# Newton steps of the first norm in runs of late priority, more buffers and one table load less, in a four-layer decoder trunk

## Chip, cores and metric

The kernel runs on one NeuronCore of one Trainium2 chip, as one program for the whole network. The metric is the device time of one execution in microseconds. Engines are named as the profile names them: PE (TensorE, with PEld for its weight loads), DVE (VectorE), ACT (ScalarE), POOL (GpSimd) and SP (SyncE, which issues the DMAs).

## What is computed

Four decoder layers of width 1024 on a sequence of 256 tokens, batch 1, all in float32. Every layer has two SwiGLU feed-forwards of half weight (hidden width 2816) around one mixer; the mixers are stick-breaking attention, MoBA, MLA and stick-breaking attention again. Cut to what matters here:

```python
def rms_norm(x, g):
    y = x * lax.rsqrt(jnp.mean(x * x, axis=-1, keepdims=True) + EPS)
    return y * g

def swiglu(x, w_gate_up, w_down):
    g, u = jnp.split(x @ w_gate_up, 2, axis=-1)
    return (jax.nn.silu(g) * u) @ w_down

h = x
for i in range(DEPTH):
    h = h + 0.5 * swiglu(rms_norm(h, norm_ffn1[i]), ffn1_w_gate_up[i], ffn1_w_down[i])
    h = h + mixer[i % 3](rms_norm(h, norm_mix[i]))
    h = h + 0.5 * swiglu(rms_norm(h, norm_ffn2[i]), ffn2_w_gate_up[i], ffn2_w_down[i])
return rms_norm(h, final_norm)
```

## The kernel before

Activations lie transposed in SBUF, features on the 128 partitions and the 256 tokens along the free axis; `h` has eight such tiles. To keep float32 accuracy at the fast matmul rate, every operand is split in two: a high part (rounded to fp32r) and a low part (what is left over). For activations they are the two halves of `x2`. For weights, `Chunk` loads up to 2048 columns into one of four `raw` buffers (SP, L315), ACT writes the high part `whi` (L320) and DVE the low part `wlo` (L327), 1024 columns at a time, into one of six pairs of part buffers (`parts`). One step of a product, here called a wide pair, is two matmuls: high weight by both halves of the activation (L478, 512 columns) and low weight by the high half (L479, 256 columns). One pair of part buffers of the gate-and-up projection feeds eight wide pairs: four contraction tiles into two PSUM banks.

A feed-forward walks over 22 groups of 128 hidden units, each with two part pairs of gate and up weights, and then over eight output tiles of the down projection. The evacuation of a group (`evac`) adds the two halves of each bank (ACT L486, DVE L487), multiplies by the row scale (L554), takes SiLU (ACT L555), multiplies (L559) and splits the result (ACT L560, DVE L561). It holds one of three intermediate buffers (`mids`) all that time.

The row scale `rb` is made by `norm_rows`: a matmul sums the squares (`sums`, L444 and L445, one wide pair), and DVE finds the reciprocal root with a first guess (L450, L451) and three Newton steps of three instructions each (L454 to L456). These eleven are one operation, `newton`. The norm gains are applied to the activations beforehand, so the matmuls don't wait for `rb`; the evacuation does.

What sets the order: every piece of work is registered as an operation with a cost, its dependencies and a priority, which is the PE time planned so far (`g.t`) minus a `lead`. `Program.emit` then plays the program through with these costs, and on each engine takes the ready operation with the lowest priority number for which buffers are free. The instructions are emitted in that order, one in-order row per engine. A higher lead means earlier. `norm_rows` has lead 10.

At the start, ACT runs a SiLU on one element (L266), which brings its function table in; the planned work then begins with a table load of its own (`table`, L467). The first three groups of weights come in small cuts.

Of the kernel before, what the change touches and what calls it, by code (L numbers as in the profile page):

```python
# [11 lines left out]
F32R = mybir.dt.float32r  # L12
BF16 = mybir.dt.bfloat16
I32 = mybir.dt.int32
AF = mybir.ActivationFunctionType
ALU = mybir.AluOpType
AX = mybir.AxisListType

P = 128
D = 1024  # L20
SEQ = 256
# [7 lines left out]
ZC = SEQ + P  # L29
EPS = 1e-6  # L30
# [9 lines left out]
HALF = MAXC // 2  # L40
# [155 lines left out]
def trunk_kernel(ctx: ExitStack, tc: tile.TileContext, a: dict, out: bass.AP, nsub: int = 3 * DEPTH):  # L196
    nc = tc.nc
# [23 lines left out]
    def room(n, shape, name, dt=F32):  # L221
        return Slots([cp.tile([P] + shape, dt, name=f"{name}{i}") for i in range(n)])
# [2 lines left out]
    raws = room(4, [MAXC], "raw")  # L225


    whi = [cp.tile([P, HALF], F32R, name=f"whi{i}") for i in range(6)]
    full = cp.tile([P, P], F32R, name="full")
    cp.tile([P, 16], F32, name="shift")  # L230

    x2 = cp.tile([P, NT, 2, SEQ], F32R, name="x2")
    a2 = cp.tile([P, NF, 2, SEQ], F32R, name="a2")
    lows = cp.tile([P, 4 + P + 6 * HALF], F32R, name="wlo")
    full_lo = lows[:, 4:4 + P]
    parts = Slots([(whi[i], lows[:, 4 + P + i * HALF:4 + P + (i + 1) * HALF]) for i in range(6)])
    mids = room(3, [2 * ZC], "mid")
    probs = room(2, [2, ZC], "prob")
    nats = room(5, [512], "nat")
    turned = room(4, [4, SEQ], "turned")  # L240
# [22 lines left out]

    zeros = nats.aps[0].bitcast(BF16)
    nc.vector.memset(nats.aps[0], 0.0)
    nc.scalar.activation(nats.aps[1][:, 0:1], nats.aps[0][:, 0:1], AF.Silu)  # L266
    for _ in range(WARM):
        nc.tensor.matmul(psum.aps[-1], zeros[:, :P], zeros[:, :512], start=True, stop=True)

# [154 lines left out]
        p = g.op("PE", 0.22, spread, [n], take=[c], lead=lead)  # L424
        return r, n, [g.act(SEQ, copy(i, s), [p], free=[c], lead=lead) for i, s in enumerate(scales)]

    def norm_rows():

        t, z = Buf(mids), bank()
        lead = 10.0

        parted = a2[:, NF - 1].rearrange("p a b -> p (a b)")
        th, tl, tx = (slice(i * SEQ, (i + 1) * SEQ) for i in range(3))

        def high():
            nc.scalar.activation(parted[:, th], acc, AF.Copy)

        def low():  # L440
            nc.vector.tensor_sub(parted[:, tl], acc, parted[:, th].bitcast(F32))

        def sums():
            nc.tensor.matmul(z.ap, full, parted, start=True, stop=False, skip_group_check=True)  # L444
            nc.tensor.matmul(z.ap[:, :SEQ], full_lo, parted[:, tl], start=False, stop=True, skip_group_check=True)  # L445

        def newton():
            x, y, u = t.ap[:, tx], t.ap[:, th], t.ap[:, tl]

            nc.vector.tensor_scalar(x, z.ap[:, :SEQ], 0.5 / D, -0.5 * EPS, op0=ALU.mult, op1=ALU.add)  # L450
            nc.vector.tensor_scalar(y.bitcast(I32), x.bitcast(I32), -0.5, float(0x1EF759DF), op0=ALU.mult,  # L451
                                    op1=ALU.add)
            for i in range(3):
                nc.vector.tensor_mul(u, y, y)  # L454
                nc.vector.tensor_mul(u, u, x)
                nc.vector.scalar_tensor_tensor(rb[:, 0, :] if i == 2 else y, u, 1.5, y, op0=ALU.add, op1=ALU.mult)  # L456

        o = g.act(SEQ, high, [state["acc"]], lead=lead)
        o = g.dve(SEQ, low, [o], lead=lead)
        o = g.op("PE", wide_cost(1), sums, [o], take=[z, t], lead=lead)  # L460
        n = g.op("DVE", 11 * 0.4, newton, [o], free=[z, t], lead=lead)
        g.act(SEQ, lambda: nc.scalar.activation(rb[:, 1, :], rb[:, 0, :], AF.Copy, scale=0.5), [n], lead=lead)
        return n

# [61 lines left out]

    def ffn(l, which, g_next):
        gu, dn = a[f"ffn{which + 1}_gu"], a[f"ffn{which + 1}_dn"]
        rms = norm_rows()
        act = [None] * NF  # L530
        xdeps = list(state["x"])

# [38 lines left out]
        for m in range(NT):  # L571
            b = bank()
            last = None
            for half in range(2):
                c = Chunk(dn[l, m, half], FH, P, 6)
                for fs in runs(FH, 3):
                    def f(fs=fs, half=half, c=c, b=b):
                        for f in fs:
                            j = half * FH + f
                            wide(b.ap, *c.get(f), a2[:, j], j == 0, j == NF - 1)  # L580
# [504 lines left out]
```

## Time and profile before

| | us |
|---|---|
| median of 3 runs | 1920.49 |
| the runs | 1920.95, 1915.59, 1920.49 |
| profiled execution | 1913.88 |
| its span in the profile | 1911.8 |
| PE busy | 1893.1 (99%) |
| DVE busy | 1467.3 (77%) |
| ACT busy | 1150.4 (60%) |

The span runs from the first to the last instruction; the 2.1 us by which the execution is longer lie around it. Matmuls overlap in the array, so the busy time of PE has no gap as long as one follows the other, and its rate is better read from the number of matmuls in a stretch. In a waits row, the engine named first sat idle until the second had delivered.

### The profile page before, as it was taken

Reading aid. Unit: us, or ns where it says so; the run is one execution under the profiler, and the core shown is the slowest. Engines: PE = TensorE matmul, PEld = TensorE weight load, DVE = VectorE, ACT = ScalarE, POOL = GpSimd, SP = SyncE. Lnnn points to the kernel's source line nnn. Section 1 sums busy time; section 2 is a strip of 40 time slices with the busy share of each in tenths; the row PEclk is TensorE's granted clock in tenths of the full one; section 3 lists DMA queues with packets and bytes.
Section 4 is the critical chain, followed back from the end, with each engine's and each line's share of the span. In section 5 each row is a group of like instructions: output and inputs, shape, how many; then the busy total and the mean of one; then the engine's idle time right before and its main releaser. Section 6 shows DMA issues by size and latency. Waiting matters only on the chain.

```text
span 1911.8 us, 30484 instructions
## 1 busy us (share of the span) xinstructions
PE 1893.1 (99%) x11649; PEld 1674.1 (88%) x11649; DVE 1467.3 (77%) x2670; ACT 1150.4 (60%) x2119; POOL 0.4 (0%) x5
## 2 busy tenths in 40 slices
PE   8999999999999999999999999999999999999997
PEld 6888989888888887988888888988888888898886
DVE  8777767876887777887787768887778777669874
ACT  6655556655656555755665657765656655666653
POOL 0000000000000000000000000000000000000000
PEclk9999999999999999999999999999999999999999
DMA  7546434545654653364655454255465456335542
GB/s 270 197 152 223 176 132 155 206 171 190 227 188 153 219 190 132 135 219 158 207 213 194 157 188 159 104 208 190 166 222 197 175 180 225 145 113 212 181 164 83
DMA packets 55873, 342.77 MB, mean 179 GB/s; under 512 B 6192, under 2 KB 7088, under 8 KB 26928
## 3 DMA queue, kind: packets, MB, share of 16 engines
q1 hardware_dynamic: 55728, 340.84, 51.3%
q8 instruction: 91, 1.49, 0.3%
q14 instruction: 54, 0.44, 0.1%
HBM read 339.76 MB, written 1.05 MB: 178 GB/s over the span
## 4 chain that ended last, share of the span: by engine, by line
PE 98%; DVE 1%; ACT 1%; DMA 0%; SPq 0%; issue 0%; DVEq 0%; ACTq 0%
PE ps L478 50%; PE ps L479 25%; PE ps L472 3%; PE ps L473 3%; PE ps L474 3%; PE ps L519 3%; PE ps L521 2%; PE ps L520 2%; PE ps L618 1%; PE ps L668 1%; PE ps L777 1%; PE ps L742 1%; PE ps L815 1%; PE ps L640 1%; PE ps L606 0%; PE ps L620 0%
## 5 line engine op out<-in xcount | busy, mean ns | idle before, releaser
L320 ACT ACTIVATE whi<-raw 128x1024 fp32r<-128x1024 f32 (+2 forms) x738 | 703.0, 954 | 659.6 <-PE ps L478 461.0
L327 DVE TENSOR_TENSOR wlo<-raw,whi 128x1024 fp32r<-128x1024 f32 (+2 forms) x738 | 803.0, 1090 | 334.8 <-ACT whi L320 315.8
L478 PE MATMUL ps<-x,whi 128*128 128x512 f32 x2816 | 962.3, 390 | 1.4 <-ACT whi L320 1.4
L479 PE MATMUL ps<-x,wlo 128*128 128x256 f32 x2816 | 779.3, 277 | 4.4 <-DVE wlo L327 4.4
L478 PEld LDWEIGHTS ps<-x,whi 128*128 128x128 f32 x2816 | 530.1, 188 | 113.2 <-ACT whi L320 2.7
L479 PEld LDWEIGHTS ps<-x,wlo 128*128 128x128 f32 x2816 | 530.0, 188 | 5.6 <-DVE wlo L327 5.5
L478 PE MATMUL ps<-a,whi 128*128 128x512 f32 x1408 | 480.1, 389 | 0.0
L479 PE MATMUL ps<-a,wlo 128*128 128x256 f32 x1408 | 388.6, 276 | 0.0
L478 PEld LDWEIGHTS ps<-a,whi 128*128 128x128 f32 x1408 | 264.3, 188 | 54.7
L479 PEld LDWEIGHTS ps<-a,wlo 128*128 128x128 f32 x1408 | 264.3, 188 | 0.0
L487 DVE TENSOR_TENSOR mid<-ps,mid 128x256 f32<-128x256 f32 x416 | 172.9, 417 | 10.0 <-ACT mid L486 9.9
L486 ACT ACTIVATE mid<-ps 128x256 f32<-128x256 f32 x416 | 151.0, 368 | 12.9 <-PE ps L479 9.9
L559 DVE TENSOR_TENSOR mid<-mid 128x256 f32<-128x256 f32 x176 | 73.9, 422 | 11.7
L554 DVE TENSOR_TENSOR mid<-mid,rb 128x256 f32<-128x256 f32 x176 | 74.1, 423 | 4.8
L555 ACT ACTIVATE mid<-mid 128x256 f32<-128x256 f32 x176 | 72.0, 410 | 7.2 <-DVE mid L554 7.2
L561 DVE TENSOR_TENSOR a<-mid,a 128x256 fp32r<-128x256 f32 x176 | 73.2, 418 | 1.1 <-ACT a L560 0.8
L519 PE MATMUL ps<-whi,x 128*128 128x512 f32 (+2 forms) x192 | 74.0, 385 | 0.0
L472 PE MATMUL ps<-a,whi 128*128 128x256 f32 x256 | 73.8, 288 | 0.0
L472 PE MATMUL ps<-x,whi 128*128 128x256 f32 x256 | 73.1, 285 | 0.0
L521 PE MATMUL ps<-whi,x 128*128 128x512 f32 (+2 forms) x192 | 72.8, 379 | 0.0
L520 PE MATMUL ps<-wlo,x 128*128 128x512 f32 (+2 forms) x192 | 72.3, 377 | 0.0
L560 ACT ACTIVATE a<-mid 128x256 fp32r<-128x256 f32 x176 | 70.6, 404 | 2.4 <-DVE mid L559 1.9
(142 smaller groups left out, 1660.2 us busy)
## 6 DMA issues: line engine op xcount, KB each, us to landing
raw<-in_ffn_gu SPq DMA_DIRECT2D x173, 1024.0 KB, 4.8
raw<-in_ffn_dn SPq DMA_DIRECT2D x128, 704.0 KB, 4.0
raw<-in_sb_qk SPq DMA_DIRECT2D x16, 1024.0 KB, 4.8
raw<-in_moba_qkv SPq DMA_DIRECT2D x12, 1024.0 KB, 4.7
raw<-in_sb_v SPq DMA_DIRECT2D x8, 1024.0 KB, 4.8
raw<-in_sb_o SPq DMA_DIRECT2D x8, 1024.0 KB, 4.8
raw<-in_moba_o SPq DMA_DIRECT2D x4, 1024.0 KB, 4.8
raw<-in_mla_o SPq DMA_DIRECT2D x4, 1024.0 KB, 4.9
```

What stands on the lines that cost most here:

```text
L320: return lambda: nc.scalar.activation(b.ap[0][:, (k - i) * w:(e - i) * w], raw.ap[:, k * w:e * w], AF.Copy)
L327: nc.vector.tensor_sub(b.ap[1][:, s], raw.ap[:, k * w:e * w], b.ap[0][:, s].bitcast(F32))
L472: nc.tensor.matmul(o, wh, mh, start=first, stop=False, skip_group_check=True)
L478: nc.tensor.matmul(o, wh, m2.rearrange("p a b -> p (a b)"), start=first, stop=False, skip_group_check=True)
L479: nc.tensor.matmul(o[:, :SEQ], wl, m2[:, 0, :], start=False, stop=last, skip_group_check=True)
L486: x = g.act(SEQ, lambda: nc.scalar.activation(o(), b.ap[:, SEQ:], AF.Copy), [last], take=take, lead=lead)
L487: return g.dve(SEQ, lambda: nc.vector.tensor_add(o(), b.ap[:, :SEQ], o()), [x], free=[b], lead=lead)
L519: nc.tensor.matmul(o, xs[0][:, k, ts], hi, start=(k == 0), stop=False)
L520: nc.tensor.matmul(o, xs[0][:, k, ts], lo, start=False, stop=False)
L521: nc.tensor.matmul(o, xs[1][:, k, ts], hi, start=False, stop=(k == n - 1))
L554: o = g.dve(SEQ, lambda: nc.vector.tensor_mul(x(), x(), rb[:, 0, :]), [o, rms])
L559: o = g.dve(SEQ, lambda: nc.vector.tensor_mul(v(), v(), x()), [o, u])
```

## The change

Five things are done. `norm_rows` registers the guess (two instructions) and the three Newton steps (three each) as four separate operations behind the sums' own. The norm of the very first feed-forward gets a lead of -16 instead of 10; all other feed-forwards keep 10. There are seven pairs of part buffers instead of six, and five intermediate buffers instead of three. The SiLU on one element at the start is gone.

```diff
-    whi = [cp.tile([P, HALF], F32R, name=f"whi{i}") for i in range(6)]
+    whi = [cp.tile([P, HALF], F32R, name=f"whi{i}") for i in range(7)]
...
-    lows = cp.tile([P, 4 + P + 6 * HALF], F32R, name="wlo")
+    lows = cp.tile([P, 4 + P + 7 * HALF], F32R, name="wlo")
     full_lo = lows[:, 4:4 + P]
-    parts = Slots([(whi[i], lows[:, 4 + P + i * HALF:4 + P + (i + 1) * HALF]) for i in range(6)])
-    mids = room(3, [2 * ZC], "mid")
+    parts = Slots([(whi[i], lows[:, 4 + P + i * HALF:4 + P + (i + 1) * HALF]) for i in range(7)])
+    mids = room(5, [2 * ZC], "mid")
...
     nc.vector.memset(nats.aps[0], 0.0)
-    nc.scalar.activation(nats.aps[1][:, 0:1], nats.aps[0][:, 0:1], AF.Silu)
...
-    def norm_rows():
+    def norm_rows(lead=10.0):
...
-        lead = 10.0
...
-        def newton():
-            x, y, u = t.ap[:, tx], t.ap[:, th], t.ap[:, tl]
-
-            nc.vector.tensor_scalar(x, z.ap[:, :SEQ], 0.5 / D, -0.5 * EPS, op0=ALU.mult, op1=ALU.add)
-            nc.vector.tensor_scalar(y.bitcast(I32), x.bitcast(I32), -0.5, float(0x1EF759DF), op0=ALU.mult,
+        x, y, u = (lambda s=s: t.ap[:, s] for s in (tx, th, tl))
+
+        def guess():
+
+            nc.vector.tensor_scalar(x(), z.ap[:, :SEQ], 0.5 / D, -0.5 * EPS, op0=ALU.mult, op1=ALU.add)
+            nc.vector.tensor_scalar(y().bitcast(I32), x().bitcast(I32), -0.5, float(0x1EF759DF), op0=ALU.mult,
                                     op1=ALU.add)
-            for i in range(3):
-                nc.vector.tensor_mul(u, y, y)
-                nc.vector.tensor_mul(u, u, x)
-                nc.vector.scalar_tensor_tensor(rb[:, 0, :] if i == 2 else y, u, 1.5, y, op0=ALU.add, op1=ALU.mult)
+
+        def newton(to):
+            def f():
+                nc.vector.tensor_mul(u(), y(), y())
+                nc.vector.tensor_mul(u(), u(), x())
+                nc.vector.scalar_tensor_tensor(to(), u(), 1.5, y(), op0=ALU.add, op1=ALU.mult)
+            return f
...
-        n = g.op("DVE", 11 * 0.4, newton, [o], free=[z, t], lead=lead)
+        n = g.dve(2 * SEQ, guess, [o], n=2, free=[z], lead=lead)
+        for i, to in enumerate((y, y, lambda: rb[:, 0, :])):
+            n = g.dve(3 * (SEQ + 60), newton(to), [n], n=3, free=[t] if i == 2 else [], lead=lead)
...
-        rms = norm_rows()
+
+        rms = norm_rows(10.0 if l or which else -16.0)
```

What this does to DVE's row in the first feed-forward, from the first evacuations on. Before (`wlo` from `whi0` is the low part for the fourth group; the Newton steps stand in one piece, of which two steps are left out here):

```order
L487 TENSOR_TENSOR mid1_90<-ps2_68,mid1_90 128x256
L450 TENSOR_SCALAR mid2_91<-ps6_72 128x256
L451 TENSOR_SCALAR mid2_91<-mid2_91 128x256
L454 TENSOR_TENSOR mid2_91<-mid2_91 128x256
...
L456 SCALAR_TENSOR_TENSOR rb_107<-mid2_91 128x256
L487 TENSOR_TENSOR mid0_89<-ps1_67,mid0_89 128x256
L554 TENSOR_TENSOR mid0_89<-mid0_89,rb_107 128x256
L487 TENSOR_TENSOR mid1_90<-ps3_69,mid1_90 128x256
L554 TENSOR_TENSOR mid1_90<-mid1_90,rb_107 128x256
L487 TENSOR_TENSOR mid2_91<-ps4_70,mid2_91 128x256
L327 TENSOR_TENSOR wlo_88<-raw3_77,whi0_78 128x1024
```

Now (the lines are shifted; L326 is the low part, L491 the add of the evacuation, L449 and L450 the guess, L455 to L457 a step; the fourth group's first low part comes from `whi6`):

```order
L439 TENSOR_TENSOR a2_88<-acc_109,a2_88 128x256
L491 TENSOR_TENSOR mid0_90<-ps1_67,mid0_90 128x256
L326 TENSOR_TENSOR wlo_89<-raw3_77,whi6_84 128x1024
L491 TENSOR_TENSOR mid1_91<-ps3_69,mid1_91 128x256
L326 TENSOR_TENSOR wlo_89<-raw3_77,whi0_78 128x1024
L326 TENSOR_TENSOR wlo_89<-raw0_74,whi1_79 128x1024
...
L449 TENSOR_SCALAR mid3_93<-ps0_66 128x256
L450 TENSOR_SCALAR mid3_93<-mid3_93 128x256
L326 TENSOR_TENSOR wlo_89<-raw1_75,whi3_81 128x1024
L491 TENSOR_TENSOR mid2_92<-ps5_71,mid2_92 128x256
L455 TENSOR_TENSOR mid3_93<-mid3_93 128x256
...
L457 SCALAR_TENSOR_TENSOR mid3_93<-mid3_93 128x256
L326 TENSOR_TENSOR wlo_89<-raw1_75,whi4_82 128x1024
```

Four low parts have moved ahead of the guess, and two more stand between the guess and the last step; the last step is followed by the low part from `whi5`, and then by ten and seven evacuation steps, each heap followed by one low part.

The first instructions of ACT, before:

```order
L266 ACT_TABLE_LOAD
L266 ACTIVATE nat_95<-nat_94 128x1
L467 ACT_TABLE_LOAD
L360 ACTIVATE x_86<-gh 128x256
L348 ACTIVATE acc<-gh 128x256
L320 ACTIVATE whi_78<-raw_74 128x256
```

and now:

```order
L471 ACT_TABLE_LOAD
L359 ACTIVATE x_87<-gh 128x256
L347 ACTIVATE acc<-gh 128x256
L319 ACTIVATE whi_78<-raw_74 128x256
L319 ACTIVATE whi_79<-raw_75 128x256
```

One load and the dummy are gone; what follows keeps its order up to the evacuations.

PE in the MLA mixer, at the end of the latents' transposes (L905, later L910), with the first transposes of a head group (L815, later L820). Before:

```order
L905 MATMUL ps_69<-identf,mid_91 128x128
L905 MATMUL ps_69<-identf,mid_89 128x128
...
L815 MATMUL ps_70<-identf,nat_95 96x128 x4
L815 MATMUL ps_66<-identf,nat_96 96x128 x4
...
L815 MATMUL ps_70<-identf,nat_97 96x128 x4
L815 MATMUL ps_66<-identf,nat_98 96x128 x4
```

and now:

```order
L910 MATMUL ps_69<-identf,mid_92 128x128
L910 MATMUL ps_69<-identf,mid_94 128x128
L820 MATMUL ps_70<-identf,nat_98 96x128 x4
...
L820 MATMUL ps_73<-identf,nat_99 96x128 x4
...
L820 MATMUL ps_70<-identf,nat_100 96x128 x4
L820 MATMUL ps_66<-identf,nat_101 96x128 x4
```

Transposes that stood together in pairs now have projections between them (left out), and the latents use a fourth and fifth intermediate buffer. Apart from this mixer, the place of the sums and the very last transposes, PE's matmuls stand in the order of before.

## Rows read from the trace of the kernel before

**Rows 1.** The page: busy time by engine, and the chain that ended last.

```profile
PE 1893.1 (99%) x11649; PEld 1674.1 (88%) x11649; DVE 1467.3 (77%) x2670; ACT 1150.4 (60%) x2119; POOL 0.4 (0%) x5
...
PE 98%; DVE 1%; ACT 1%; DMA 0%; SPq 0%; issue 0%; DVEq 0%; ACTq 0%
```

**Rows 2.** Stretches: length, busy time (instructions) by engine, PE clock, DMA share, GB/s.

```profile
0.00:20.00 20.00, 16.94 (x71) 11.83 (x72) 15.43 (x38) 16.38 (x34) 0.44 (x5) 0.91 0.86 304
20.00:40.00 20.00, 15.85 (x83) 13.64 (x82) 16.87 (x34) 11.86 (x21) 0.00 (x0) 0.91 0.53 196
40.00:60.00 20.00, 20.00 (x119) 17.78 (x118) 16.92 (x27) 12.47 (x22) 0.00 (x0) 1.00 0.77 289
```

**Rows 3.** The waits of PE, longest first: total us, times, longest us.

```profile
PE ps L479 <- DVE wlo L327: 4.4, 2, 4.2
PE ps L378 <- ACT nat L379: 2.3, 1, 2.3
PE ps L268 <- DVE nat L265: 1.5, 1, 1.5
PE ps L478 <- ACT whi L320: 1.4, 2, 1.2
PE ps L815 <- ACT nat L205: 0.7, 2, 0.4
```

**Rows 4.** Timeline of PE around its longest wait: start us, us, instruction, wait.

```profile
25.52 0.39 PE L478 MATMUL ps<-x,whi 128*128 128x512 f32 x1
...
25.86 0.39 PE L478 MATMUL ps<-x,whi 128*128 128x512 f32 x1
30.40 0.39 PE L479 MATMUL ps<-x,wlo 128*128 128x256 f32 x1 [4.15 <-DVE wlo L327]
...
36.03 0.39 PE L478 MATMUL ps<-x,whi 128*128 128x512 f32 x1
```

**Rows 5.** Timeline of DVE and ACT in the same stretch.

```profile
19.84 0.95 DVE L487 TENSOR_TENSOR mid<-ps,mid 128x256 f32<-128x256 f32 x2
20.22 1.05 ACT L320 ACTIVATE whi<-raw 128x1024 fp32r<-128x1024 f32 x1
22.66 0.42 DVE L450 TENSOR_SCALAR mid<-ps 128x256 f32<-128x256 f32 x1 [1.88 <-PE ps L445]
...
27.47 0.41 DVE L487 TENSOR_TENSOR mid<-ps,mid 128x256 f32<-128x256 f32 x1
27.80 0.41 DVE L554 TENSOR_TENSOR mid<-mid,rb 128x256 f32<-128x256 f32 x1
...
29.14 1.21 DVE L327 TENSOR_TENSOR wlo<-raw,whi 128x1024 fp32r<-128x1024 f32 x1
...
36.11 3.49 DVE L327 TENSOR_TENSOR wlo<-raw,whi 128x1024 fp32r<-128x1024 f32 x3
```

**Rows 6.** Stretches around the two falls of PE's granted clock.

```profile
11.10:14.50 3.40, 3.40 (x13) 2.82 (x12) 3.37 (x8) 3.37 (x9) 0.00 (x0) 0.50 1.05 391
26.20:30.40 4.20, 0.05 (x1) 0.00 (x1) 4.12 (x10) 2.75 (x7) 0.00 (x0) 1.00 0.03 12
31.60:35.00 3.40, 3.40 (x13) 2.92 (x12) 3.36 (x6) 1.17 (x3) 0.00 (x0) 0.50 0.25 34
```

**Rows 7.** Timeline of ACT at the start.

```profile
0.73 1.28 ACT L266 ACT_TABLE_LOAD   x1 [0.73 <-PEq L1069]
...
2.25 1.28 ACT L467 ACT_TABLE_LOAD   x1
3.54 0.51 ACT L360 ACTIVATE x<-gh 128x256 fp32r<-128x256 f32 x1
...
6.79 0.42 ACT L320 ACTIVATE whi<-raw 128x256 fp32r<-128x256 f32 x1 [0.47 <-DMA raw<-in_ffn_gu]
```

**Rows 8.** Stretches of the MLA mixer, columns as in rows 2.

```profile
1160.00:1180.00 20.00, 19.34 (x116) 17.16 (x115) 16.44 (x50) 15.02 (x34) 0.00 (x0) 1.00 0.61 195
1180.00:1200.00 20.00, 19.62 (x128) 15.94 (x127) 17.87 (x65) 15.72 (x52) 0.00 (x0) 1.00 0.31 118
```

## Prediction

> **What bounds the kernel now.** I read the views in this order: the busy shares, the stretches of 20 us, the waits of TensorE, then the order of time around the longest wait. TensorE (PE) is busy for 99% of the span and carries 98% of the chain that ended last [rows 1]. From 40 us on nothing is left to take: between 40 and 60 us 119 matmuls fit into 20 us and PE is never idle [rows 2]. Only the first 40 us differ. Between 20 and 40 us there are 83 matmuls, 36 fewer, and the granted clock averages 0.91 [rows 2]. The waits of PE say why: one wait for a low weight part (`wlo`, made by VectorE, DVE) lasts 4.2 us, and apart from the two ends of the program (1.5 us for the first zeros, 2.3 us in the last norm) no other exceeds 1.2 us [rows 3].
>
> In order of time the place is plain. At full speed one wide pair of matmuls (L478 and L479) starts every 0.34 us (25.52 to 25.86). The L478 at 25.86 is followed by an L479 only at 30.40, and the twelfth L478 after it starts at 36.03 [rows 4]. Twelve pairs should take 12 x 0.34 = 4.08 us; they took 36.03 - 25.86 = 10.17. **The hole costs 6.1 us.** About 4.4 of it is the wait with its restart; the rest, 1.7, goes in the stretch from 31.6 to 35.0 us, where the granted clock is 0.50 (1.2 GHz) after PE had stood idle [rows 6].
>
> Why `wlo` was late: DVE finished its ready work at 20.8, sat idle for 1.88 us until PE delivered the sums, and then ran all eleven Newton instructions in one piece, from 22.66 to 27.47. Five evacuation steps follow, and only at 29.14 comes the `wlo` for which PE had stopped [rows 5]. ScalarE (ACT) had made the matching `whi` at 20.22 [rows 5], so the input was there eight microseconds earlier. Order on DVE, not capacity, made the hole.
>
> **The change, part by part.**
>
> Newton in runs, late. The eleven instructions stay; what moves is when they stand in DVE's row. In the new order the low part of the sums comes after two adds, and four `wlo` (raw3 twice, raw0 twice) stand ahead of the first guess; two more `wlo` and two adds stand between guess and steps, as the listing of the change shows. I walk that row with durations of before: 4.81 us for eleven Newton instructions (22.66 to 27.47), 0.33 us for one evacuation step (27.47 to 27.80), 3.49 / 3 = 1.16 us for one `wlo` of 1024 columns [rows 5]. PE eats one pair of part buffers in 8 x 0.34 = 2.72 us [rows 4]. It asks for the part that was late at about 26.1 minus 0.34, since the sums (one wide pair) no longer stand ahead of it: 25.75. Take a late start for it on DVE, 22.66, where Newton stood: it ends at 23.8, 1.9 us early. From there to the sixth next `wlo` DVE has four adds, eleven Newton instructions and six `wlo`: 1.3 + 4.8 + 7.0 = 13.1 us, so it is done at 36.9. PE asks for that one at 25.75 + 0.34 + 6 x 2.72 = 42.4. The two after it stand behind ten and seven evacuation steps: 41.4 against 45.2, and 44.9 against 47.9. Each arrives early, by 1.9 us at the least. So the wait goes, and with it the idle stretch ahead of the half-speed one: -6.1 us if both go, -4.4 if the wait alone goes. I take -6.1, the row. What is late next is nothing in this stage: per group of two parts DVE needs 2 x 1.16 + 5 x 0.33 = 4.0 us against 5.44 of PE.
>
> What is queued behind Newton's result: it is now ready some 7 us later (about 35 instead of 27.47), and the SiLU steps of the first four groups wait for it. They hold four of the five intermediate buffers and Newton the fifth; with three buffers as before, the evacuation would have stood still. That is what the two added buffers buy, and without them the cover of the walk above is gone. Later feed-forwards keep the early priority (lead 10); their Newton was hidden before (PE waits nowhere there [rows 3]) and splitting it only puts other work between its steps: 0.
>
> Seven pairs of part buffers. PE already eats without a gap from 40 us on [rows 2]; a seventh pair lets DVE and ACT run 2.7 us further ahead there and is worth 0. Within the first stage it is the pair that the late group uses, and it is counted above. SP's queue keeps its order, and its weight loads can only start earlier as raw buffers come free earlier: 0.
>
> One table load less. ACT's first load takes 1.28 us, a dummy SiLU follows, and the second load ends at 3.53; the first real work starts at 3.54 [rows 7]. Removed: about 1.5 us of ACT, at once. But at 6.79 ACT stands idle for 0.47 us until the weights land [rows 7], and that landing does not move, so what is won before it is lost there: 0, with -0.3 as the other end (the first input may land a little ahead of 3.54) and no loss, since the work is only taken away.
>
> MLA. PE's matmuls keep their order everywhere but around the sums, at the very end, and in the MLA mixer, where five intermediates let both latents be held at once, so projections and transposes are interleaved differently. PE's idle time in that stage is 0.66 + 0.38 us in 1160 to 1200 [rows 8]; that is the most it can win. I take 0, with -1.0 and +1.0 as ends (as much new waiting as there was).
>
> A row on the clock: the half-speed stretches are 11.1 to 14.5 us, after a start in which PE waits for data, and 31.6 to 35.0, after the long wait [rows 6]. The first stays, since nothing moves there. The Trainium skill (TensorE: Matmul & The Clock Gate, section "What's actually happening") says that activity releases a default throttle and that its window runs freely, not tied to the kernel's start. The trace agrees that idle time came before each; by that rule the 1.7 us would be paid in some executions and not, or twice, in others, which one profile cannot show, and the sum would be anywhere between -4.4 and -7.8. The sum stays with the row.
>
> **Sum.** -6.1 + 0 + 0 + 0. The profiled execution took 1913.88 us, its span 1911.8 and 2.1 around it, so the same execution would take 1907.8. The median of the three runs is 1920.49, 6.6 above that profile; the runs spread from 1915.59 to 1920.95, so about 0.3% is what a measurement can tell from no change, here 5.8 us. Against the median: 1920.49 - 6.1 = **1914.4 us**, a gain of 0.32%, just over that bound.
>
> **Rivals.**
>
> The wait goes, the half-speed loss does not: the clock falls for another pause of the start (it did at 11.1 us after short waits), or the median run never paid it. Gain 4.4: 1916.1. For it: the first such stretch has no long wait ahead of it. (By the Trainium skill's page above, some executions would be spared it.) Against it: PE has no pause left between 11 and 40 us in my walk. Within 0.3%.
>
> The wait moves: late Newton puts 17 evacuation steps in a heap between 35 and 45 us, and if ACT's SiLU steps hold DVE there by more than the 3 us of margin, PE stops for a `wlo` there instead. A stop of the same length gives 1920.5, half of it some 1917.5. For it: DVE is 85% busy there already (16.92 of 20 us [rows 2]). Against it: the margin is 1.9 to 5.5 us everywhere.
>
> Slower: MLA's new interleaving makes PE wait for copies. DVE is busy for 17.87 of 20 us there, PE's present waits are up to 0.4 us for one group of transposes [rows 3, 8]. If each of its 16 groups (4 head groups, queries and keys, two token halves) waited 0.4 us more, it would cost 6.4 and eat the gain: 1920.8. It decides from 0.38 us a group on; slower by over 0.3% takes 0.74 us each. Against it: in the new order five copies go from DVE to ACT, and no count of work grows.
>
> The change doesn't do what it says: Newton could still stand ahead of the `wlo`. The new order excludes it.
>
> **How the numbers follow.** Forecast 0.68, wait alone 0.15, moved wait 0.12, MLA 0.05. The forecast's own time lies near the 5.8 us bound, so I count some 0.72 of it as faster by over 0.3%, since the slower runs may hold more half-speed time than the profile; with a tenth of the wait-alone and moved cases (a faster median) that gives 0.52 for faster. Slower by over 0.3% takes most of an MLA heap: 0.03. The rest, 0.45, is within. The range: down by the -1.3 of start and MLA, one more half-speed stretch (1.7) and part of the 4.9 us by which one of the runs lies under their median: 1908. Up to the wait-alone case and most of the moved one, with the MLA end: 1919.
>
> **What would show it.** In the profile after: 20 to 40 us holds near 119 matmuls; no wait of PE for `wlo` above 1 us; clock 1.00 from 15 us to the end; on DVE `wlo` between guess and steps. ACT has one load before its first real work, which starts near 3.2, and still waits for weights near 6.8. MLA's PE idle stays near 1 us. Wrong would be: PE waiting for `wlo` between 35 and 48 us (moved wait), a half-speed stretch after 20 us without a pause (the clock), or over 5 us of new PE waits in MLA.

## The result, and the profile after

The changed kernel takes 1906.02 us (median; 1905.5 to 1907.2), the kernel before in the same comparison 1919.97 (1915.6 to 1921.0): 14 us apart. The ratio on record for these runs is 0.9941, interval 0.992 to 0.9962; the two medians alone would give 0.9927. The direction was forecast, with a gain of 6.1 us. The two profiled executions are nearer to each other: 1906.4 against 1913.88 us, spans 1904.6 against 1911.8. So there are two things to explain: 7.2 us of span, and why the medians differ by almost twice that.

The page of after, busy time by engine and the chain that ended last, answers to [rows 1]:

```profile
PE 1890.6 (99%) x11649; PEld 1674.4 (88%) x11649; DVE 1463.4 (77%) x2665; ACT 1144.7 (60%) x2122; POOL 0.4 (0%) x5
...
PE 99%; ACT 0%; DVE 0%; DMA 0%; SPq 0%; issue 0%; DVEq 0%; ACTq 0%
```

The stretches of after, columns as in [rows 2]; they answer to [rows 2], [rows 6] (the second one) and [rows 8]:

```profile
0.00:20.00 20.00, 16.68 (x76) 12.46 (x77) 15.00 (x37) 15.23 (x34) 0.44 (x5) 1.00 0.87 299
11.10:14.50 3.40, 3.32 (x20) 2.95 (x20) 3.37 (x9) 3.40 (x10) 0.00 (x0) 1.00 1.04 383
20.00:40.00 20.00, 20.00 (x120) 17.74 (x119) 19.02 (x37) 15.39 (x24) 0.00 (x0) 1.00 0.73 287
40.00:60.00 20.00, 20.00 (x120) 17.74 (x119) 19.12 (x35) 13.53 (x28) 0.00 (x0) 1.00 0.66 217
1160.00:1180.00 20.00, 19.99 (x128) 18.21 (x127) 18.13 (x52) 16.35 (x42) 0.00 (x0) 1.00 0.54 200
1180.00:1200.00 20.00, 20.00 (x141) 16.52 (x140) 18.34 (x61) 16.16 (x51) 0.00 (x0) 1.00 0.29 106
```

Between 20 and 40 us PE now does 120 matmuls instead of 83 and is never idle. In MLA its two idle bits, 0.66 and 0.38 us, are gone as well. The granted clock is 1.00 in every one of these stretches, also from 11.1 to 14.5 us, where the profile of before had 0.50.

All waits of PE in after (total us, times, longest us), against [rows 3]:

```profile
PE ps L377 <- ACT nat L378: 2.3, 1, 2.3
PE ps L482 <- DVE acc L350: 1.6, 1, 1.6
PE ps L267 <- DVE nat L265: 1.5, 1, 1.5
PE ps L483 <- DVE wlo L326: 0.2, 1, 0.2
```

The wait of 4.2 us for `wlo` is gone and none of its kind has come: the one wait for a `wlo`, of 0.2 us, lies in the first 15 us, and before had the same one there. What is left is the start of the program and the last norm.

DVE's row in after around the place, against [rows 5]:

```profile
22.64 3.48 DVE L326 TENSOR_TENSOR wlo<-raw,whi 128x1024 fp32r<-128x1024 f32 x3
...
26.60 0.42 DVE L449 TENSOR_SCALAR mid<-ps 128x256 f32<-128x256 f32 x1
27.06 0.29 DVE L450 TENSOR_SCALAR mid<-mid 128x256 int32<-128x256 int32 x1
27.27 1.22 DVE L326 TENSOR_TENSOR wlo<-raw,whi 128x1024 fp32r<-128x1024 f32 x1
...
29.99 1.22 DVE L326 TENSOR_TENSOR wlo<-raw,whi 128x1024 fp32r<-128x1024 f32 x1
...
33.62 0.43 DVE L457 SCALAR_TENSOR_TENSOR rb<-mid 128x256 f32<-128x256 f32 x1
33.96 1.22 DVE L326 TENSOR_TENSOR wlo<-raw,whi 128x1024 fp32r<-128x1024 f32 x1
35.10 1.09 DVE L559 TENSOR_TENSOR mid<-mid,rb 128x256 f32<-128x256 f32 x3
```

Where before eleven Newton instructions stood in one piece, four `wlo` now come ahead of the guess (three in the first row shown, one at 21.17) and others between guess, runs and what follows. Newton's result (`rb`) is ready at 34.0 us instead of 27.5, and the steps that need it follow from 35.10.

ACT at the start of after, against [rows 7]:

```profile
0.73 1.28 ACT L471 ACT_TABLE_LOAD   x1 [0.73 <-PEq L1074]
3.15 0.51 ACT L359 ACTIVATE x<-gh 128x256 fp32r<-128x256 f32 x1 [1.14 <-DMA gh<-in_gx]
...
5.01 0.42 ACT L319 ACTIVATE whi<-raw 128x256 fp32r<-128x256 f32 x1 [0.74 <-DMA raw<-in_ffn_gu]
...
7.16 0.42 ACT L319 ACTIVATE whi<-raw 128x256 fp32r<-128x256 f32 x1 [0.69 <-DMA raw<-in_ffn_gu]
```

ACT's first real work starts 0.39 us earlier than before (3.15 against 3.54), and ACT then waits for data three times: the load that was saved became waiting.

Set side by side by the start of the k-th wide pair of matmuls, the two profiles part in four places. By the 20th pair after is 0.82 us ahead (its first data landed later, which cost 0.8, but it had no half-speed stretch). From the 32nd to the 64th pair the lead grows from 0.82 to 6.91: **the hole, 6.09 us**. Then the lead does not move for 2575 pairs. MLA adds 0.91 (7.82 behind it), and the last norm gives 0.6 back: 7.2 us of span.

The 0.6 us at the end are a matter of the clock. Two of PE's last six matmuls in before and, second row, the same two in after:

```profile
1902.84 0.44 PE L378 MATMUL ps<-identf,nat 128*128 128x128 f32 x2 [2.30 <-ACT nat L379]
1895.02 0.69 PE L377 MATMUL ps<-identf,nat 128*128 128x128 f32 x2 [2.30 <-ACT nat L378]
```

In after the granted clock falls to 0.50 at 1894.8 us, ahead of these matmuls; in before it falls at 1905.5, behind them. The four that follow take 0.85 us instead of 0.50. The prediction's sign of a clock of 1.00 "from 15 us to the end" thus holds only up to the last norm.

### The profile page after: what moved, and what is told of

The parts are those of the page before. It is cut to its first block, busy times and chain, and to the rows that moved or that the text cites. A ratio compares the mean times of both kernels' runs of the same rounds, so it can differ in the third digit from the quotient of the medians.

```text
span 1904.6 us, 30475 instructions
## 1 busy us (share of the span) xinstructions
PE 1890.6 (99%) x11649; PEld 1674.4 (88%) x11649; DVE 1463.4 (77%) x2665; ACT 1144.7 (60%) x2122; POOL 0.4 (0%) x5
## 4 chain that ended last, share of the span: by engine, by line
PE 99%; ACT 0%; DVE 0%; DMA 0%; SPq 0%; issue 0%; DVEq 0%; ACTq 0%
PE ps L482 50%; PE ps L483 25%; PE ps L476 3%; PE ps L477 3%; PE ps L478 3%; PE ps L523 3%; PE ps L525 3%; PE ps L524 3%; PE ps L623 1%; PE ps L673 1%; PE ps L820 1%; PE ps L782 1%; PE ps L747 1%; PE ps L645 1%; PE ps L611 0%; PE ps L625 0%
## 5 line engine op out<-in xcount | busy, mean ns | idle before, releaser
L326 DVE TENSOR_TENSOR wlo<-raw,whi 128x1024 fp32r<-128x1024 f32 (+2 forms) x738 | 803.0, 1089 | 319.7 <-ACT whi L319 317.2
L483 PE MATMUL ps<-x,wlo 128*128 128x256 f32 x2816 | 778.0, 276 | 0.2 <-DVE wlo L326 0.2
L491 DVE TENSOR_TENSOR mid<-ps,mid 128x256 f32<-128x256 f32 x416 | 173.5, 417 | 13.1 <-ACT mid L490 12.3
L490 ACT ACTIVATE mid<-ps 128x256 f32<-128x256 f32 x416 | 151.3, 366 | 13.3 <-PE ps L483 13.2
L478 PE MATMUL ps<-x,wlo 128*128 128x256 f32 x256 | 71.9, 281 | 0.0
```

Of the source, the lines that this page charges most:

```text
L326: nc.vector.tensor_sub(b.ap[1][:, s], raw.ap[:, k * w:e * w], b.ap[0][:, s].bitcast(F32))
L478: nc.tensor.matmul(o, wl, mh, start=False, stop=last, skip_group_check=True)
L483: nc.tensor.matmul(o[:, :SEQ], wl, m2[:, 0, :], start=False, stop=last, skip_group_check=True)
L490: x = g.act(SEQ, lambda: nc.scalar.activation(o(), b.ap[:, SEQ:], AF.Copy), [last], take=take, lead=lead)
L491: return g.dve(SEQ, lambda: nc.vector.tensor_add(o(), b.ap[:, :SEQ], o()), [x], free=[b], lead=lead)
```

## The experiments

Two theories for the medians stood at the start. **A** put the extra gain on the clock: the executions of before that take 1920 us hold more half-speed time than the profiled one, and the change takes that away too. **B** left the change its 6 us and took the heap at 1920 for something that has nothing to do with the hole, so that it would show up in any kernel. Each comparison below runs the kernel before on the same chip beside the others.

### The kernel before, once more

No edit.

> The kernel before, unchanged but for an empty line at its end: a measure of how its executions spread and of their clock. The timed median before (1919.97) lies 6.1 us above its own profiled execution (1913.88), while the changed kernel's median (1906.02) lies 0.4 under its profile. Theory A (the hole at 26 to 36 us costs more in most executions than in the one that was profiled, through more half-speed time): the mean granted clock of the timed executions is lower than 0.9966, the profile's, by 0.001 to 0.003, that is 4 to 12 us more at half speed. Theory B (the surplus lies in the waits or the transfers of the start or in MLA and not in the clock): the clock stays at 0.9966 in all of them, and the times still spread over 5 us. Ratio 1.000 within 0.003 by both.

The ratio was 1.0001 (0.9987 to 1.0015). The times do not spread, they fall into two heaps: of its 12 executions eight took 1912.9 to 1915.3 us and four 1919.8 to 1920.3. The runs of before beside it, 35, did the same: 25 in 1912.4 to 1915.5 (mean 1913.6), 10 in 1918.9 to 1921.8 (mean 1920.0), and nothing between. The mean granted clock is 0.996 to 0.998 in the upper heap and 0.996 or 0.997 in the lower. A loss of 6.4 us to half speed would take 12.8 us at 0.50, which lowers the mean by 0.003; it is not lower. This speaks against A; what the heaps are is told by the next runs.

### The Newton part with five intermediate buffers

Of the change only the runs of late priority and the five buffers (with three, Newton and the steps that hold the buffers would wait for each other in a ring, so that case has no run):

```diff
-    whi = [... for i in range(7)]            # after
+    whi = [... for i in range(6)]
-    parts = Slots([... for i in range(7)])
+    parts = Slots([... for i in range(6)])
+    nc.scalar.activation(nats.aps[1][:, 0:1], nats.aps[0][:, 0:1], AF.Silu)
```

> Newton's part of the change with the five intermediate buffers that it needs; six pairs of part buffers and the dummy SiLU with its table load are kept as before. Theory A: it has the whole gain of the change but MLA's 0.9 us: no wait of PE for the low part at 26 us, time 1905.5 to 1909, ratio 0.994 to 0.9955. Theory B: only the hole's own 6.1 us go, ratio 0.9965 to 0.9975, and the other 5 us show up with the parts or the table load.

Ratio 0.9968 (0.9954 to 0.9983). Again two heaps: eight executions in 1906.2 to 1909.2 (mean 1907.3), four in 1913.3 to 1915.2 (mean 1914.2). Heap against heap that is 6.3 and 5.8 us less than before: the Newton part is the forecast's 6.1. The profiled execution was one of the upper heap and shows what the heaps are. Stretches of this kernel:

```profile
20.00:40.00 20.00, 20.00 (x115) 17.27 (x114) 18.34 (x37) 13.79 (x22) 0.00 (x0) 1.00 0.71 287
40.00:60.00 20.00, 20.00 (x115) 17.27 (x114) 18.21 (x32) 12.89 (x26) 0.00 (x0) 1.00 0.58 211
```

and of the kernel before as run above:

```profile
40.00:60.00 20.00, 20.00 (x119) 17.70 (x119) 17.40 (x27) 12.06 (x22) 0.00 (x0) 1.00 0.75 278
```

PE is busy for all 20 us in both, the clock is 1.00 in both, and yet 115 matmuls fit in one and 119 in the other. PE's timeline shows the step from pair to pair. The kernel with the Newton part:

```profile
99.85 0.40 PE L483 MATMUL ps<-x,whi 128*128 128x512 f32 x1
100.09 0.28 PE L484 MATMUL ps<-x,wlo 128*128 128x256 f32 x1
100.21 0.40 PE L483 MATMUL ps<-x,whi 128*128 128x512 f32 x1
...
101.27 0.40 PE L483 MATMUL ps<-x,whi 128*128 128x512 f32 x1
```

The kernel before:

```profile
99.65 0.39 PE L478 MATMUL ps<-x,whi 128*128 128x512 f32 x1
99.88 0.28 PE L479 MATMUL ps<-x,wlo 128*128 128x256 f32 x1
99.99 0.39 PE L478 MATMUL ps<-x,whi 128*128 128x512 f32 x1
...
101.01 0.39 PE L478 MATMUL ps<-x,whi 128*128 128x512 f32 x1
```

Four pairs take 1.42 us in the first and 1.36 in the second: **0.353 us a pair against 0.340**, with the same instructions, no wait and the same clock. I call them the long and the short pace. Here the long pace held from the start until the mixer at about 200 us. Over the first feed-forward's 460 to 500 pairs 13.3 ns each are 6.1 to 6.7 us, the distance of the heaps. Not everything runs slower in the long pace: between 60 and 180 us a weight load of PE takes 187 ns on average here and 188 in the profile of after (short pace), and a `wlo` of 1024 columns 1225 and 1224 ns; the matmuls of 512 columns are recorded with 397 against 389 ns.

### All but the Newton part

Seven pairs of parts, five buffers, no first table load; Newton as before:

```diff
-        n = g.dve(2 * SEQ, guess, [o], n=2, free=[z], lead=lead)
-        for i, to in enumerate((y, y, lambda: rb[:, 0, :])):
-            n = g.dve(3 * (SEQ + 60), newton(to), [n], n=3, ...)
+        n = g.op("DVE", 11 * 0.4, newton, [o], free=[z, t], lead=lead)
```

> The change without Newton's part: seven pairs of part buffers, five intermediates, no dummy SiLU and table load; Newton stays one early run of eleven. Theory A: the wait at 26 us stays at about 4 us with a half-speed stretch behind it, gain only MLA's 0.9 us: ratio 0.9985 to 1.000. Theory B: this has some 5 us of the gain: ratio 0.997 to 0.998.

Ratio 0.9994 (0.9981 to 1.0007): nine in 1911.75 to 1913.4 (mean 1912.3), three in 1919 to 1920.9. The hole stays, as the waits of PE say:

```profile
PE ps L478 <- DVE wlo L326: 4.4, 2, 4.2
```

The profiled execution is again of the upper heap, and this time the pace changed within it: 0.340 us a pair up to the hole (25.13, 25.47, 25.81), and behind it

```profile
29.50:36.30 6.80, 4.92 (x16) 4.24 (x17) 6.44 (x13) 4.17 (x9) 0.00 (x0) 0.50 0.14 34
40.00:60.00 20.00, 20.00 (x115) 17.25 (x115) 17.90 (x28) 11.27 (x19) 0.00 (x0) 1.00 0.84 309
```

115 matmuls, the long pace. The first row shows a second thing that is drawn by the execution: the half-speed stretch behind the hole is 6.8 us here, of which PE is busy for 4.9, and was 3.4 in [rows 6].

### Seven pairs of part buffers alone

```diff
-    whi = [... for i in range(6)]            # before
+    whi = [... for i in range(7)]
-    lows = cp.tile([P, 4 + P + 6 * HALF], F32R, name="wlo")
+    lows = cp.tile([P, 4 + P + 7 * HALF], F32R, name="wlo")
-    parts = Slots([... for i in range(6)])
+    parts = Slots([... for i in range(7)])
```

> Seven pairs of part buffers alone. The planned order changes in MLA and not in the mixers before it. By the walk on rows nothing is won before 40 us; in MLA PE's 1.0 us of waits goes, as in the trace of the changed kernel: -0.9 us, ratio 0.999 to 1.000 (Theory A). If MLA's short waits also cost clock in timed executions (Theory B): ratio 0.997 to 0.998. The hole at 26 us stays by both.

Ratio 0.9999 (0.9987 to 1.0011). The one place where it differs is MLA; its two stretches there:

```profile
1160.00:1180.00 20.00, 20.00 (x118) 18.05 (x117) 17.77 (x53) 15.57 (x32) 0.00 (x0) 1.00 0.62 216
1180.00:1200.00 20.00, 19.99 (x139) 16.83 (x139) 19.09 (x63) 17.32 (x58) 0.00 (x0) 1.00 0.38 143
```

PE's 1.04 us of idle time are gone, and from the last pair ahead of MLA to the first behind it it gains 0.91 us, as in the changed kernel. The kernel with five buffers and six pairs kept 19.35 and 19.63 there and gained 0.05. So the seventh pair, not the two added buffers, makes the gain in MLA. It is read from the profiles: the times alone, with an interval of 0.0012 to either side, could not tell it from nothing. With these runs the second half of theory B falls as well: the other 5 us show up neither with the parts nor with the table load. Heap against heap the seven pairs alone gain 0.2 and 0.6 us, all but the Newton part 1.3 and 0.0.

### The changed kernel, once more

The observations led to theory **P**: after a pause of PE it is chance which pace sets in, and it stays until the next mixer. Against it stood **Q**: the new build itself holds the short pace, which would explain why no execution of after was in the upper heap so far. No edit.

> The changed kernel, unchanged but for an empty line. The traces so far show two paces of PE in the first feed-forward after its last pause: a wide pair every 0.340 us or every 0.353, and the one that sets in stays to the first mixer (some 460 to 500 pairs, 6.2 to 6.7 us). Theory P (which pace sets in is chance at every pause and has nothing to do with the change): about a third of the executions lie 6 to 7 us above the others, as before the change, and fast against fast the change gives the hole's 6.1 and MLA's 0.9: 1905.5 to 1907, ratio 0.9955 to 0.997. Theory Q (the change also keeps the slow pace away): all executions lie within 3 us, median 1906, ratio 0.994 to 0.9955.

Ratio 0.9969 (0.9956 to 0.9982). Four executions took 1906.2 to 1907.5 us, eight 1912.0 to 1914.5: P. The profiled one was of the upper heap, and its stretches are those of the long pace up to the mixer and of the short one in the second feed-forward:

```profile
40.00:60.00 20.00, 20.00 (x115) 17.30 (x114) 18.42 (x35) 13.39 (x28) 0.00 (x0) 1.00 0.57 190
...
420.00:440.00 20.00, 20.00 (x120) 17.68 (x119) 13.11 (x26) 11.39 (x22) 0.00 (x0) 1.00 0.45 145
```

The runs of before beside it: 20 up to 1915.5 (mean 1914.2), 14 from 1919 (mean 1920.0). Heap against heap the change gives 1914.2 - 1906.8 = 7.4 and 1920.0 - 1913.2 = 6.8 us. In the first comparison three of four executions of before had fallen into the upper heap and none of the four of after.

### The table load put back

The changed kernel with the dummy SiLU of before.

```diff
+    nc.scalar.activation(nats.aps[1][:, 0:1], nats.aps[0][:, 0:1], AF.Silu)
```

> The changed kernel with the dummy SiLU and its table load put back. By the prediction (ACT waits for the weights at 6.8 us anyway) nothing: within 1 us of the changed kernel when executions of one pace are compared, ratio to before 0.9955 to 0.997. If the load costs the 1.5 us that it takes on ACT: 0.0008 more.

Ratio 0.9961 (0.9946 to 0.9975); lower heap of seven at 1905.3 to 1907.6 (mean 1906.2, against 1906.8 without it), upper heap of five at 1912.0 to 1914.8. The load costs nothing that shows.

### Late, but in one run

The changed kernel with Newton in one piece of eleven, at the late priority.

```diff
+        n = g.op("DVE", 11 * 0.4, newton, [o], free=[z, t], lead=lead)   # lead is -16
```

> The changed kernel, but Newton is one operation of eleven instructions again, still with late priority (lead -16). Theory late (the priority alone moves the low parts ahead): no hole, same time as the changed kernel within 0.5 us. Theory split (the runs are needed, since eleven instructions in a row take 4.8 us and the margin is 1.9 to 5.5): a wait of PE for a low part between 28 and 45 us of 0.5 to 3 us, with half-speed time behind it, 1 to 5 us slower than the changed kernel.

Ratio 0.9961 (0.9947 to 0.9975): six at 1906.3 to 1908.6 (mean 1907.5), five at 1912.2 to 1914.5. Lateness alone brings the gain but for some 0.7 us, which need not be a loss of the kernel: three of the six lie at 1906.3 to 1906.8 with a mean granted clock of 0.998, three at 1908.3 to 1908.6 with 0.997. Neither theory met it: the wait is there, but shorter than 0.5 us and without half-speed time behind it. PE's timeline has one pause, where a `wlo` came a little late:

```profile
38.45 0.39 PE L476 MATMUL ps<-x,whi 128*128 128x512 f32 x1
38.68 0.28 PE L477 MATMUL ps<-x,wlo 128*128 128x256 f32 x1
38.79 0.39 PE L476 MATMUL ps<-x,whi 128*128 128x512 f32 x1
39.32 0.38 PE L477 MATMUL ps<-x,wlo 128*128 128x256 f32 x1
39.54 0.39 PE L476 MATMUL ps<-x,whi 128*128 128x512 f32 x1
...
39.89 0.40 PE L476 MATMUL ps<-x,whi 128*128 128x512 f32 x1
...
40.25 0.40 PE L476 MATMUL ps<-x,whi 128*128 128x512 f32 x1
```

From 38.79 to 39.54 one pair takes 0.75 us instead of 0.34. The steps ahead of it are 0.34, those behind it 0.35 to 0.36: a pause of 0.4 us was followed by the other pace.

### In runs, but early

```diff
-        rms = norm_rows(10.0 if l or which else -16.0)
+        rms = norm_rows(10.0)
```

> The changed kernel, Newton in runs, but with the old early priority (lead 10). Theory late: the runs don't help, as each is ready soon after the one ahead and still goes first; PE waits some 1 to 4 us for low parts between 23 and 31 us; slower than the changed kernel by 2 to 6 us. Theory split: the low parts slip between the runs, no wait above 0.5 us, same time as the changed kernel.

Ratio 0.9969 (0.9955 to 0.9982): nine at 1908.0 to 1910.9 (mean 1909.3), three at 1914.9 to 1917.5. Splitting alone brings 4.9 of the 7.4 us, MLA's 0.9 among them; the waits of PE show what stays:

```profile
PE ps L483 <- DVE wlo L326: 2.3, 3, 1.4
```

Two pauses, at the 48th and the 56th pair, in the place of one.

### Two more Newton steps in the kernel before

In the first norm alone, which lengthens the piece on DVE by six instructions (and sharpens the root a little).

```diff
-            for i in range(3):
+            for i in range(5 if first else 3):
```

> The kernel before, with five Newton steps instead of three in the first norm alone (six more instructions of 0.46 us on DVE, still in one early run). If Newton's place on DVE makes the hole, PE's wait for the low part grows from 4.2 by 2.7 us to 6.9, the time by 2.7 (up to 3.4 more with a longer half-speed stretch): ratio 1.001 to 1.003. If something else holds the low part (its raw data or its high part), the wait stays near 4.2 and the ratio at 1.000.

Ratio 1.0042 (1.0026 to 1.0058). The wait in question:

```profile
PE ps L479 <- DVE wlo L327: 7.0, 2, 6.8
```

4.2 became 6.8; six instructions of 4.81 / 11 us are 2.6. PE waits for Newton's piece to end, instruction for instruction. The time rose by more, and the ratio lies above the 1.001 to 1.003 that was expected: two executions at 1916.9 and 1917.9 and four at 1922.8 to 1924.8 (mean 1924.0) stand against heaps of before with means of 1913.2 and 1919.4, so 4.2 and 4.5 us more. Against the profile of before, this one loses 3.1 us between the 32nd and the 64th pair: the 2.6 and some 0.4 of half-speed time, since PE runs at 0.50 from 34.2 to 38.2 us, 4.1 us instead of 3.4. Another 0.9 is lost ahead of that, at the start, where PE waits 2.0 us instead of 1.2 for a `whi`; the prolonged piece has no part in that.

### A pause of PE in the second feed-forward

The changed kernel with 37 idle instructions on DVE ahead of an evacuation in the second feed-forward, to stop PE there. P expects a new draw of the pace; its rival **S** ties the long pace to the start of the program.

```diff
+            if l == 0 and which == 1 and j == 8:
+                ...
+                def pause(hold=hold):
+                    nc.vector.memset(hold.ap[:, :SEQ], 0.0)
+                    for _ in range(36):
+                        nc.vector.tensor_mul(hold.ap[:, :SEQ], hold.ap[:, :SEQ], hold.ap[:, :SEQ])
+                g.op("DVE", 0.5, pause, [act[5]], take=[hold], free=[hold], lead=20.0)
```

> The changed kernel with 36 idle instructions on DVE, a memset and 36 products of zeros, put into the second feed-forward of the first layer (some 16.6 us), so that PE has to pause there for some 5 us. Theory P (any pause of PE draws its pace anew, and the pace then holds to the next mixer): in some third to two thirds of the executions wide pairs run at 0.353 us from there to the second mixer, some 430 pairs or 5.7 us, so that the times form up to three heaps, 0, 6 and 12 us above about 1913 (the changed kernel plus the pause and some half-speed time); a profile shows 0.340 or 0.353 there. Theory S (the slow pace is something of the program's start alone): pairs at 0.340 behind the pause in every execution, and two heaps as for the changed kernel.

Ratio 1.0028 (1.001 to 1.0045), in three heaps: five at 1912.3 to 1914.5, two at 1920.3 and 1920.6, five at 1924.8 to 1926.1. The wait of PE, and stretches ahead of it, at its end and behind it:

```profile
PE ps L482 <- DVE mid L491: 4.9, 1, 4.9
```

```profile
330.00:350.00 20.00, 20.00 (x119) 17.68 (x119) 16.93 (x31) 11.63 (x22) 0.00 (x0) 1.00 0.59 211
...
366.00:370.00 4.00, 3.67 (x12) 3.14 (x13) 3.86 (x7) 3.01 (x7) 0.00 (x0) 0.57 0.73 254
370.00:390.00 20.00, 20.00 (x115) 17.28 (x114) 19.27 (x34) 15.27 (x29) 0.00 (x0) 1.00 0.70 235
...
660.00:680.00 20.00, 20.00 (x115) 17.31 (x114) 14.31 (x22) 11.31 (x17) 0.00 (x0) 1.00 0.71 245
```

The short pace ahead of the pause, the long one behind it, up to the second mixer at 683 us, and the short one behind that. Against the profile of after the loss grows from 8.0 us at the 695th pair, where the half-speed stretch ends, to 19.9 at the mixer: 889 pairs of some 13.4 ns, 11.9 us. P had counted 430 pairs and 5.7 us, since it overlooked that no mixer stands between this feed-forward and the first of the next layer. 11.9 us is about the distance from the lowest heap to the highest, and the middle one lies where the long pace in the first feed-forward alone would put it. P holds in its main point, a pause far from the start can bring the long pace; S falls. The opposite step is on record too: in the profiles of the kernel before run again, of the seven pairs alone and of the five Newton steps the pace is 0.353 from 17 us up to the hole and 0.340 from 39 us on.

### Small matmuls in the way

If a mixer brings the short pace back, perhaps other matmuls do. The changed kernel with eight matmuls of zeros, 128 columns each, ahead of the sixth group of the first feed-forward; run twice.

```diff
+            if l == 0 and which == 0 and j == 5:
+                ...
+                    for _ in range(8):
+                        nc.tensor.matmul(spare.ap[:, :P], zeros[:, :P], zeros[:, :P], start=True, stop=True)
```

> The changed kernel with eight small matmuls (128 columns of zeros, 0.5 us or less in all, into a bank that nobody reads) on PE ahead of the sixth group of the first feed-forward. After each mixer, which has many small matmuls, PE has always been seen at 0.340 us a pair. If such matmuls bring the slow pace back to the fast one, all executions lie within 3 us at 1906 to 1908 (the changed kernel's fast heap plus 0.5), ratio 0.994 to 0.996. If they don't, some third to two thirds of the executions stay 6 to 7 us above, as with the changed kernel, ratio 0.996 to 0.9975.

> The same kernel with the eight small matmuls once more, for more executions: five of five lay at 1905.5 to 1907.8, where the changed kernel alone had eight of twelve at 1912 to 1914.5 on another chip and none of four on a third. If the small matmuls bring the slow pace back, all executions lie below 1909, ratio to before 0.994 to 0.9965, and a profile that begins at 0.353 us a pair changes to 0.340 behind them. If five of five was chance, a quarter or more of the executions lie above 1911.

The first time all five executions lay at 1905.5 to 1907.8 (ratio 0.9961, 0.9949 to 0.9973), the second time nine at 1905.9 to 1908.2 and three at 1912.8 to 1914.9 (ratio 0.9964, 0.9952 to 0.9976). The second time's profiled execution had the long pace on both sides of the small matmuls, which start at 38.53 us (the first row is 18 us long, in which the first profile of after has 108 matmuls):

```profile
20.00:38.00 18.00, 18.00 (x103) 15.55 (x102) 15.80 (x29) 12.48 (x20) 0.00 (x0) 1.00 0.81 312
40.00:60.00 20.00, 20.00 (x115) 17.30 (x114) 18.54 (x33) 12.79 (x27) 0.00 (x0) 1.00 0.54 190
```

So they do not bring the short pace back; five of five had been chance. None of the kernels tried is shown to be better than the changed one.

## Why the prediction was right, and where it was off

**The hole, right.** Forecast 6.1 us with its half-speed stretch, measured 6.09 between the two profiles, and some 6 heap against heap with the Newton part alone (6.3 and 5.8). That the first two agree so closely says only that the whole hole is gone, as both are read from the same execution of before; in the two other profiles where the stretch at 0.50 lasts 6.8 us, the place costs some 0.8 more. That is less than the 1.7 by which the prediction got to -7.8, because part of the stretch falls into PE's pause (4.92 us busy of 6.80). The cause was Newton's place on DVE: with everything else changed the wait stays at 4.2 us, with six more instructions it grows by 2.6. The walk along DVE's row held: behind 15 us PE waits for no `wlo` at all (of its sums one is off by 0.1: 42.4 + 2.72 is 45.1 and not 45.2, which decides nothing). `rb` came at 34.0 us where the walk had about 35. Of lateness and runs either alone takes most of the hole away; lateness alone leaves a pause of 0.4 us, runs alone two of 1.4 and 0.7. That the gain is the wait alone (4.4) or that the wait moves is excluded by 120 matmuls between 20 and 40 us at a clock of 1.00.

**The table load, right.** 0, with the reason given: ACT's saved time became waits for data.

**MLA, mis-sized within its bounds.** I took 0, it gave 0.9, close to the end of -1.0, which was all of PE's idle time there. The reason was wrong as well: I put the new interleaving down to the five buffers, but the seventh pair of parts does it alone. I had priced that pair at 0 for the feed-forwards, where it is 0, and never asked for MLA.

**The first half-speed stretch, wrong.** "The first stays, since nothing moves there": in the profile of after it is missing. It belongs to the execution, not to the kernel: the changed kernel's second profile has a granted clock of 0.52 from 11.1 to 14.5 us, its first 1.00, and the seven pairs alone, with the start of before, 1.00. The Trainium skill (TensorE: Matmul & The Clock Gate, "What's actually happening") states that the window of the clock gate runs freely and is not reset when a kernel starts. What the prediction worked out from that, stretches that come in some executions and not in others, agrees with these rows and with the 3.4 and 6.8 us behind the hole. The sum should have left that 1.6 us open in both directions.

**The step that failed: from the profile to the median.** The sum by itself gave 1907.8 us for an execution like the profiled one; it took 1906.4 (-0.9 MLA, -0.8 start, +0.6 last norm at half speed, -0.3 around the span). Then I carried the gain over to the median of 1920.49, 6.6 us above the profile, and took the distance for spread and for half-speed time. It was neither: the profiled execution was of the lower heap and two of the three runs shown of the upper one. The pace is a term of 6 to 7 us that the sum did not have, drawn anew in each execution and present in both kernels. Had the medians been drawn alike, 1920 would have become 1913, some 1.4 under the forecast; with after in the lower heap it became 1906.02, below the 1908 at which my range ended. The chance for "faster" came out of a bound of 0.3% and a gain of 0.32%, which was fair for heap against heap (0.36 to 0.39%); the 0.59% of the first comparison is larger than what the change brings, and that it came out so clearly was the luck of the draw.

## What to carry to other kernels

When one engine feeds another in program order, a chain of small dependent steps set at high priority can stop the fed engine while ready work waits behind it; set it as late as its own readers allow, and count the buffers that its readers hold meanwhile. Before a gain of a few tenths of a per cent is read from medians, list all executions: if they lie in heaps, compare heap with heap, and do not carry a sum made in one heap to a median of another. A buffer added for one stage should be priced in every stage that draws on the same pool.

## What the runs showed of the hardware

- **Two paces at one granted clock.** A pair of matmuls (128x512 and 128x256) starts every 0.340 or every 0.353 us with PE 100% busy and the clock at 1.00; 20 us hold 119 to 120 or 115 of them. Either can follow a pause of PE (as short as 0.4 us, at 38.79 us) and then stays; in every profile the pace behind a mixer was 0.340. It costs 6 to 7 us in the first feed-forward and 11.9 where it lasted from 367 to 683 us. What decides it, and why the mixers end it, stays open; eight small matmuls do not.
- **Half-speed time is drawn too.** At the same pause of some 4 us the stretch at 0.50 was 3.4 us in two profiles and 6.8 in two others (some 0.8 us dearer, as it began within the pause), and the one at 11.1 us comes and goes between executions of one kernel.
